# A matmul with a decayed running sum: w in four parts, the last group's upper half chunk by chunk, and output halves that rotate

## The chip, the core and the metric

The kernel runs on one core of one Trainium2 chip. The metric is the device time of an execution in microseconds (us); I quote medians of several executions. A profile is one execution, so its span can differ from the median by a us or two (932.1 against 934.55 for the kernel before). A ratio is the mean time of one kernel's runs over the mean time of the kernel before in the same rounds on the same chip, so it is not quite the ratio of the medians that I quote. Engines in the profile: PE is TensorE (matmul), PEld its weight loads, DVE VectorE, ACT ScalarE, POOL GpSimd, SP SyncE.

## The reference

```python
B, S, D = (16, 2048, 1024)
xw = x @ w
out[:, 0, :] = xw[:, 0, :]
for t in range(1, S):
    out[:, t, :] = decay[None, :] * out[:, t - 1, :] + xw[:, t, :]
```

## The kernel before: the parts that matter

The 16 x 2048 rows of x are cut into 64 chunks of 512 time steps, and chunks go in groups of two. A chunk is loaded by GpSimd's DMA queue, which casts to bf16 (the queue counts 68.18 MB for x and half of w, half of their 136.3 MB in f32), turned by a 32x32 transpose on VectorE ("turn", 2.3 us), and copied to matmul layout, mostly by ScalarE ("part"). TensorE then makes eight output tiles per group, n = 0 to 7, each from eight slots k of w. Behind each tile, ScalarE, GpSimd and VectorE do the recurrence (three tiles of four on every second time step, "paired", with a `scan` on half the steps), and VectorE transposes the result back into the output buffer `ot`, from which SyncE stores.

What the change touches is the start, the end and `ot`:

```python
groups = [[c, c + 1] for c in range(0, nch - 2, 2)] + [[nch - 2], [nch - 1]]

def ot_tile():
    return ring(sb, "ot", 2, [128, 2 * NJ, CQ])       # both halves of the columns
# ... cut ...
def lower(m):                                         # w's lower columns, f32, SyncE
    for q in range(NQ):
        pin(nc.sync.dma_start(out=stage[quad(q), m],
            in_=_ap(w, [[2 * D, P], [D, 2], [1, CH]], (q * CQ + m * 2 * P) * D)))
def upper(m):                                         # upper columns, cast to bf16, GpSimd
    for q in range(NQ):
        pin(nc.gpsimd.dma_start(out=stage2[quad(q), m], in_=...))
# ... cut ...
lower(0)
# decay: eight strided loads from ScalarE's queue
# x chunk 0 in two halves
for m in range(1, M):
    lower(m)
# x chunk 1 in two halves
for m in range(M):
    upper(m)
# ... cut ...
for m in range(M):
    at(m // 2, settle, m, 1, [nc.vector.tensor_copy] * 2)   # upper half into matmul layout
# ... cut ...
loads.extend((c, q) for c in (2, 3, 4) for q in range(NQ))  # later chunks, between GpSimd's adds
```

Of the kernel before, what the change touches and what calls it, by code (L numbers as in the profile page):

```python
# [25 lines left out]
def kernel(  # L26
# [25 lines left out]

    nc = tc.nc
# [4 lines left out]
    NQ = 4  # L58
# [26 lines left out]
    groups = [[c, c + 1] for c in range(0, nch - 2, 2)] + [[nch - 2], [nch - 1]]  # L85
    for g in groups:
        assert chunks[g[0]][0] == chunks[g[-1]][0]
# [6 lines left out]
    def ot_tile():  # L94
        return ring(sb, "ot", 2, [128, 2 * NJ, CQ])
# [29 lines left out]
    def matmul(ps, n, k, xt, t0=0, t1=TL):  # L125
        pin(nc.tensor.matmul(  # L126
            out=ps[:, t0:t1],
            lhsT=wsb[:, k, n].rearrange("p q i -> p (q i)"),
            rhs=xt[:, k // 2, k % 2, t0:t1],
            start=(k == 0),  # L130
            stop=(k == K - 1),
        ))
# [3 lines left out]
    class Tile:  # L136
# [3 lines left out]
        def __init__(self, gi, n, ps, ot):  # L140
            g = groups[gi]
# [3 lines left out]
            self.final = gi + 1 == len(groups)  # L145
            if len(g) == 2:
                self.paired = n % 4 != 3
            else:
                self.paired = n % 2 == 0 and not (self.final and n == K - 2)
# [65 lines left out]
        def back(self):  # L215
            T, n = self.T, self.n
            pin(nc.vector.transpose(  # L217
                out=self.ot[:, :, n * P:(n + 1) * P],
                in_=self.so[:, 2:T + 2].rearrange("p (i t) -> p i t", t=P)))
            if n == 3:  # L220
                self.store(0, 4)
            elif n == 5 and self.final:
                self.store(4, 6)
            elif n == 7:
                self.store(6 if self.final else 4, 8)

        def store(self, n0, n1):
            for q in (0, 2, 1, 3):
                pin(nc.sync.dma_start(
                    out=_ap(out, [[D, P], [P * D, self.T // P], [1, (n1 - n0) * P]],  # L230
                            (self.b * S + self.t0) * D
                            + n0 // R * CH + q * CR + n0 % R * P),
                    in_=self.ot[quad(q), :, n0 * P:n1 * P]))


    room = ot_tile().rearrange("p j c -> p (j c)")
    stage = room[:, 0:K * CH].rearrange("p (m e d) -> p m e d", m=M, e=2)
    stage2 = room[:, K * CH:K * CH * 3 // 2].bitcast(BF16).rearrange(
        "p (m e d) -> p m e d", m=M, e=2)

    def lower(m):
        for q in range(NQ):
            pin(nc.sync.dma_start(
                out=stage[quad(q), m],
                in_=_ap(w, [[2 * D, P], [D, 2], [1, CH]], (q * CQ + m * 2 * P) * D)))

    def upper(m):
        for q in range(NQ):
            pin(nc.gpsimd.dma_start(  # L249
                out=stage2[quad(q), m],  # L250
                in_=_ap(w, [[2 * D, P], [D, 2], [1, CH]], (q * CQ + m * 2 * P) * D + CH)))

    def settle(m, h, copies):
        for e, copy in enumerate(copies):
            src = (stage, stage2)[h][:, m, e]
            pin(copy(out=wcols[:, 2 * m + e, h],  # L256
                     in_=src.rearrange("p (q r i) -> p q r i", q=NQ, r=R)))

    def cast(m):
        settle(m, 0, (nc.vector.tensor_copy, nc.scalar.copy))  # L260

    idle = const.tile([128, TL], BF16, name="idle")
    spare = ring(psp, "spare", 1, [128, TL])
    pin(nc.vector.memset(idle, 0.0))  # L264
    for _ in range(40):
        pin(nc.tensor.matmul(out=spare, lhsT=idle[:, 0:128], rhs=idle, start=True, stop=True))  # L266
    H = NJ // 2
    halves = ((0, H), (H, NJ))
    lower(0)
    with nc.allow_non_contiguous_dma(reason="a vector of 1024"):  # L270
        for q in range(NQ):
            for h in range(2):
                pin(nc.scalar.dma_start(
                    out=dec[quad(q), h * R:(h + 1) * R],
                    in_=_ap(decay, [[1, P], [P, R]], h * CH + q * CR)))
# [3 lines left out]
    pin(nc.gpsimd.memset(stage[:, 1:M, 0, 0:1], 0.0))  # L279
    for m in range(1, M):  # L280
        lower(m)
# [3 lines left out]
    for m in range(M):  # L285
        upper(m)
# [6 lines left out]
    for m, (j0, j1) in enumerate(halves):  # L293
        enter(0, j0, j1)
        cast(m)
    for m in range(2, M):
        cast(m)
    pin(nc.vector.tensor_tensor(out=dec2[:, 0:K], in0=dec, in1=dec, op=ALU.mult))
    for j0, j1 in halves:
        enter(1, j0, j1)  # L300

# [12 lines left out]
    for m in range(M):  # L314
        at(m // 2, settle, m, 1, [nc.vector.tensor_copy] * 2)
    steps = {2: (3, 3, 4), 3: (4, 5, 6), 4: (7, 8, 10), nch - 1: (-11, -10, -8)}
    for gi, g in enumerate(groups):
        for l, c in enumerate(g):
            if c > 1:
                ahead = (-7, -6, -4) if l or len(g) == 1 else (-11, -10, -8)  # L320
                ahead = [gi * K + s for s in ahead]
                when = steps.get(c, ahead)
                if c == nch - 1:
                    when = [gi * K + s for s in when]
# [25 lines left out]
    loads.extend((c, q) for c in (2, 3, 4) for q in range(NQ))  # L350
    for gi, g in enumerate(groups):
        T = TL * len(g)
        if len(g) == 2:
            ot = ot_tile()
        else:
            if g[0] == nch - 2:
                both = ot_tile()
            ot = both[:, g[0] % 2 * NJ:(g[0] % 2 + 1) * NJ]
        heads = []
        if gi == 0:  # L360
            heads = [ring(psp, "ps", 3, [128, T]) for _ in range(3)]
            firsts = [ps[:, 0:TL] for ps in heads] + [spare]
            for k in range(K):
                for n in range(R):
                    matmul(firsts[n], n, k, xt_of[0])
            for j0, j1 in halves:
                for n in range(2):
                    for k in range(K):
                        matmul(heads[n][:, TL:T], n, k, xt_of[1], j0 * P, j1 * P)
        for n in range(K):  # L370
            if gi == 0 and n < R:
                if n < 3:
                    ps, second = heads[n], heads[n][:, TL:T]
                else:
                    second = ring(psp, "ps", 3, [128, TL])
                    ps = (spare, second)
                if n >= 2:
                    for k in range(K):
                        matmul(second, n, k, xt_of[1])
            else:  # L380
                if len(g) == 2 or n % 4 < 3:
                    ps = ring(psp, "ps", 3, [128, T])
                else:
                    ps = ring(psp, "spare", 1, [128, TL])
                for k in range(K):
                    for l, c in enumerate(g):
                        matmul(ps[:, l * TL:(l + 1) * TL], n, k, xt_of[c])
            behind(Tile(gi, n, ps, ot))
            for f in agenda.pop(gi * K + n, []):
                f()  # L390
            for _ in range(2 if len(loads) > NQ else 1):
                if loads:
                    load(*loads.pop(0))
# [31 lines left out]
```

## Time and profile before

| | before |
|---|---|
| median of four executions | 934.55 us (932.65 to 934.96) |
| span of the profiled one | 932.1 us |
| first useful matmul | 14.74 us |
| last matmul ends | 920.5 us |
| from there to the end of the span | 11.6 us |
| GpSimd's queue carries | x and half of w: 68.18 MB |
| SyncE's queue carries | half of w and all stores: 136.33 MB |

TensorE works without a gap from about 168 us to 920 us. The time is therefore decided before 168 us and after 920 us.

### The profile page before, as it was taken

The numbers are of one execution on the slowest core, as the hardware profiler recorded it, in microseconds if no ns is written. First come the engines' busy times: TensorE is split into PE (matmuls) and PEld (weight loads), VectorE is DVE, ScalarE is ACT, GpSimd is POOL, SyncE is SP. The second block draws the span as 40 slices with busy tenths as digits, with TensorE's granted clock in tenths as the row PEclk, the third lists the DMA queues.
The fourth block names the chain that finished last, engine by engine and source line by source line (L and its number), as shares of the span: only waits on it lengthen the run. The fifth ranks groups of instructions, "written<-read, shape, count | busy, mean of one in ns | idle before, by whom it ended". The sixth has DMA issues, their size and how long they took to land. (4 is left out here: it accounts for less than half of the span.)

```text
span 932.1 us, 11965 instructions
## 1 busy us (share of the span) xinstructions
PE 902.6 (97%) x4152; PEld 407.6 (44%) x4152; DVE 829.5 (89%) x613; ACT 685.9 (74%) x945; POOL 668.2 (72%) x767
## 2 busy tenths in 40 slices
PE   7879999999999999999999999999999999999995
PEld 2424444444444444444444444444444444444442
DVE  2869997999999999999999999999999999998997
ACT  2368877777877877877877777787787787787662
POOL 5867877777677777767777777777877777775542
PEclk9989999999999999999999999999999999999998
DMA  9899999999999999999999999999999999999678
GB/s 187 109 185 200 215 220 235 244 248 248 248 246 253 234 225 228 232 223 235 227 223 233 227 224 233 232 222 231 229 229 229 229 234 222 229 231 192 156 170 192
DMA packets 407548, 205.27 MB, mean 220 GB/s; under 512 B 14272, under 2 KB 406464, under 8 KB 407488
## 3 DMA queue, kind: packets, MB, share of 16 engines
q1 hardware_dynamic: 269760, 136.33, 59.9%
q0 software_dynamic: 136576, 68.18, 55.1%
q8 instruction: 32, 0.52, 0.2%
q10 hardware_dynamic: 1152, 0.00, 0.1%
q14 instruction: 28, 0.23, 0.1%
HBM read 138.42 MB, written 134.22 MB: 292 GB/s over the span
## 5 line engine op out<-in xcount | busy, mean ns | idle before, releaser
L126 PE MATMUL ps<-xt,wsb 128*128 128x512 bf16 x4072 | 883.8, 380 | 16.7 <-DVE wsb L256 5.2
L126 PEld LDWEIGHTS <-wsb 128*128 128x128 bf16 x4112 | 403.1, 98 | 504.7 <-issue 19.9
L176 POOL TENSOR_TENSOR xs<-h,xs 128x512 f32<-128x512 f32 (+1 forms) x193 | 246.8, 1279 | 194.2 <-ACT h L160 89.5
L217 DVE STREAM_TRANSPOSE ot<-so 128x1024 f32<-128x1024 f32 (+1 forms) x264 | 302.8, 1184 | 10.1 <-DMA out_dram<-ot 7.5
L170 ACT COPY xs<-ps 128x1024 f32<-128x1024 f32 (+1 forms) x193 | 192.2, 996 | 153.6 <-PE ps L126 150.9
L210 POOL TENSOR_TENSOR so<-h,xs 128x512 f32<-128x512 f32 (+1 forms) x193 | 245.6, 1273 | 47.4 <-ACT h L160 24.0
L123 ACT COPY xt<-xw 128x2048 bf16<-128x2048 bf16 (+1 forms) x128 | 240.0, 1876 | 18.2 <-DVE xw L115 18.2
L160 ACT ACTIVATE h<-so,dec 128x512 f32<-128x512 f32 (+1 forms) x193 | 147.6, 765 | 51.5 <-DVE so L182 47.7
L105 POOL DMA_DIRECT2D xb<-in_x_dram x264 | 174.6, 662 | 4.8 <-DMA xb<-in_x_dram 2.4
L115 DVE STREAM_TRANSPOSE xw<-xb 128x2048 f32<-128x2048 f32 (+1 forms) x66 | 146.7, 2222 | 14.3 <-DMA xb<-in_x_dram 14.2
L182 DVE TENSOR_TENSOR_SCAN so<-dec,xs 128x512 f32<-128x512 f32 x96 | 117.2, 1221 | 33.5 <-POOL xs L176 30.3
L182 DVE TENSOR_TENSOR_SCAN so<-dec,keep,xs 128x512 f32<-128x512 f32 (+1 forms) x97 | 120.1, 1238 | 29.9 <-POOL xs L176 29.8
L160 ACT ACTIVATE h<-ps,dec 128x512 f32<-128x512 f32 (+1 forms) x193 | 132.3, 686 | 0.0
L196 DVE TENSOR_TENSOR_SCAN so<-dec,keep,ps 128x1024 f32<-128x1024 f32 (+1 forms) x35 | 75.8, 2169 | 0.0
L196 DVE TENSOR_TENSOR_SCAN so<-dec,ps 128x1024 f32<-128x1024 f32 x31 | 70.1, 2261 | 0.0
L213 ACT COPY keep<-so 128x1 f32<-128x1 f32 x136 | 25.4, 187 | 0.2 <-DVE so L196 0.2
L175 ACT COPY so<-keep 128x1 f32<-128x1 f32 x97 | 18.5, 191 | 0.0
L249 POOL DMA_DIRECT2D ot<-in_w_dram x16 | 9.2, 579 | 6.9 <-DMA xb<-in_x_dram 6.7
L266 PE MATMUL spare<-idle 128*128 128x512 bf16 x40 | 11.5, 461 | 1.2 <-DVE idle L264 1.2
L173 POOL MEMSET so<- 128x1 f32 x96 | 11.3, 118 | 0.0
L126 PE MATMUL spare<-xt,wsb 128*128 128x512 bf16 x40 | 10.6, 379 | 0.0
L256 DVE CAST wsb<-ot 128x512 bf16<-128x512 f32 x4 | 1.7, 427 | 7.9 <-DMA ot<-in_w_dram 7.9
(15 smaller groups left out, 25.9 us busy)
## 6 DMA issues: line engine op xcount, KB each, us to landing
out_dram<-ot SPq DMA_DIRECT2D x248, 512.0 KB, 10.1
xb<-in_x_dram POOLq DMA_DIRECT2D x248, 256.0 KB, 7.6
out_dram<-ot SPq DMA_DIRECT2D x12, 256.0 KB, 4.2
ot<-in_w_dram SPq DMA_DIRECT2D x16, 128.0 KB, 6.5
xb<-in_x_dram POOLq DMA_DIRECT2D x16, 128.0 KB, 7.7
ot<-in_w_dram POOLq DMA_DIRECT2D x16, 64.0 KB, 3.0
out_dram<-ot SPq DMA_DIRECT2D x8, 128.0 KB, 2.7
dec<-in_decay_dram ACTq DMA_DIRECT2D x8, 0.5 KB, 4.7
```

Source lines behind the costliest of these rows:

```text
L105: pin(nc.gpsimd.dma_start(out=xb_of[c][quad(q), j0:j1], in_=_ap(x, [[D, P], [P * D, j1 - j0], [1, CQ]], (b * S + t0 + j0 * P) * D + q * CQ)))
L115: pin(nc.vector.transpose(out=dst.rearrange("p (m j i) -> p j m i", m=M, i=P)[:, j0:j1], in_=src.rearrange("p (j m c) -> p j m c", m=M, c=P)))
L123: pin(copy(out=xt_of[c][:, m0:m1, :, j0 * P:j1 * P], in_=src))
L126: pin(nc.tensor.matmul(out=ps[:, t0:t1], lhsT=wsb[:, k, n].rearrange("p q i -> p (q i)"), rhs=xt[:, k // 2, k % 2, t0:t1], start=(k == 0), ...
L160: pin(nc.scalar.activation(out=h, in_=src, func=mybir.ActivationFunctionType.Copy, scale=dec[:, self.n:self.n + 1]))
L170: pin(nc.scalar.copy(out=self.xs, in_=self.ps))
L176: pin(nc.gpsimd.tensor_tensor(out=self.xs[:, 1:T:2], in0=g, in1=self.xs[:, 1:T:2], op=ALU.add))
L182: pin(nc.vector.tensor_tensor_scan(out=so[:, 3:T + 2:2], data0=dec2[:, n:n + 1].to_broadcast([128, T // 2]), data1=self.xs[:, 1:T:2], init ...
L196: pin(nc.vector.tensor_tensor_scan(out=so[:, t:t + size], data0=dec[:, n:n + 1].to_broadcast([128, size]), data1=ps, initial=before, op0=A ...
L210: pin(nc.gpsimd.tensor_tensor(out=so[:, 2:T + 2:2], in0=h, in1=self.xs[:, 0:T:2], op=ALU.add))
L213: pin(nc.scalar.copy(out=self.keep, in_=so[:, T + 1:T + 2]))
L217: pin(nc.vector.transpose(out=self.ot[:, :, n * P:(n + 1) * P], in_=self.so[:, 2:T + 2].rearrange("p (i t) -> p i t", t=P)))
```

## The change

The intent: the first matmuls need only half of w's slots and half a chunk of x; w comes as (lower, even slots) by SyncE, then (lower, odd), (upper, even) and (upper, odd) by GpSimd in between the chunks of x, each part in four large loads. Decay comes contiguous, after w's first part. The third chunk of x is loaded before GpSimd's first add. Each half of the output columns has its own buffer. The last group is a pair for its lower columns and single chunks for its upper ones. A GpSimd memset that kept SyncE's later pieces of w behind the first loads of x (it ran at 6.01 us) goes. The diff, cut to its core:

```diff
-    groups = [[c, c + 1] for c in range(0, nch - 2, 2)] + [[nch - 2], [nch - 1]]
+    groups = [[c, c + 1] for c in range(0, nch, 2)]
-    def ot_tile():
-        return ring(sb, "ot", 2, [128, 2 * NJ, CQ])
+    def ot_tile(nj):
+        return ring(sb, "ot", 4, [128, nj, CR])
...
+    def load_w(queue, h, e):
+        for q in range(NQ):
+            pin(queue.dma_start(
+                out=stage[h, e][quad(q)].rearrange("p (m d) -> p m d", m=M),
+                in_=_ap(w, [[2 * D, P], [2 * P * D, M], [1, CH]],
+                        (q * CQ + e) * D + h * CH)))
...
-    for _ in range(40):
+    for _ in range(34):
...
-    lower(0)
-    (eight strided loads of decay by ScalarE)
+    load_w(nc.sync, 0, 0)
+    (four contiguous loads of decay by SyncE, into rows)
     (x chunk 0, two halves)
-    pin(nc.gpsimd.memset(stage[:, 1:M, 0, 0:1], 0.0))
-    for m in range(1, M):
-        lower(m)
+    load_w(nc.gpsimd, 0, 1)
     (x chunk 1, two halves)
-    for m in range(M):
-        upper(m)
+    load_w(nc.gpsimd, 1, 0)
+    load_w(nc.gpsimd, 1, 1)
+    for q in range(NQ):
+        load(2, q)
...
-        at(m // 2, settle, m, 1, [nc.vector.tensor_copy] * 2)
+        at(0, settle, 1, 1, m, nc.vector.tensor_copy)
-    steps = {2: (3, 3, 4), 3: (4, 5, 6), 4: (7, 8, 10), nch - 1: (-11, -10, -8)}
+    steps = {2: (3, 3, 4), 3: (4, 5, 5), 4: (7, 8, 10)}
...
-    loads.extend((c, q) for c in (2, 3, 4) for q in range(NQ))
+    loads.extend((c, q) for c in (3, 4) for q in range(NQ))
+    slots = [(g, n) for g in groups[:-1] for n in range(K)]
+    slots += [(groups[-1], n) for n in range(R)]
+    slots += [([c], n) for c in groups[-1] for n in range(R, K)]
...
+            for j0, j1 in halves:
+                for k in range(0, K, 2):
+                    for i in range(R):
+                        matmul(firsts[i], i, k, xt_of[0], j0 * P, j1 * P)
+            for k in range(1, K, 2):
+                for i in range(R):
+                    matmul(firsts[i], i, k, xt_of[0])
```

More of the change, by code (lines that the diff above doesn't have):

```diff
@@ L84 @@
     nch = len(chunks)
-    groups = [[c, c + 1] for c in range(0, nch - 2, 2)] + [[nch - 2], [nch - 1]]
+    groups = [[c, c + 1] for c in range(0, nch, 2)]
     for g in groups:
-        assert chunks[g[0]][0] == chunks[g[-1]][0]
+        assert chunks[g[0]][0] == chunks[g[1]][0]
     dec = const.tile([128, K], FP32, name="dec")
@@ L123, in part, with matmul @@
         pin(copy(out=xt_of[c][:, m0:m1, :, j0 * P:j1 * P], in_=src))
-    def matmul(ps, n, k, xt, t0=0, t1=TL):
+    def matmul(ps, n, k, xt, t0=0, t1=TL, start=0):
         pin(nc.tensor.matmul(
@@ L129, in matmul @@
             rhs=xt[:, k // 2, k % 2, t0:t1],
-            start=(k == 0),
+            start=(k == 0 and t0 == start),
             stop=(k == K - 1),
@@ L136, with __init__ @@
     class Tile:
-        def __init__(self, gi, n, ps, ot):
-            g = groups[gi]
+        def __init__(self, g, n, ps, ot):
             self.b, self.t0 = chunks[g[0]]
@@ L144, in __init__ @@
             self.n, self.ps, self.ot = n, ps, ot
-            self.final = gi + 1 == len(groups)
+            self.final = g == [nch - 1]
             if len(g) == 2:
-                self.paired = n % 4 != 3
+                self.paired = n % R != R - 1
             else:
@@ L217, in back @@
             pin(nc.vector.transpose(
-                out=self.ot[:, :, n * P:(n + 1) * P],
+                out=self.ot[:, :, n % R * P:(n % R + 1) * P],
                 in_=self.so[:, 2:T + 2].rearrange("p (i t) -> p i t", t=P)))
-            if n == 3:
-                self.store(0, 4)
-            elif n == 5 and self.final:
-                self.store(4, 6)
-            elif n == 7:
-                self.store(6 if self.final else 4, 8)
+            if self.final:
+                if n % 2:
+                    self.store(n - 1, n + 1)
+            elif n % R == R - 1:
+                self.store(n + 1 - R, n + 1)
@@ L227, in store @@
         def store(self, n0, n1):
+            c0 = n0 % R * P
+            size = (n1 - n0) * P
             for q in (0, 2, 1, 3):
                 pin(nc.sync.dma_start(
-                    out=_ap(out, [[D, P], [P * D, self.T // P], [1, (n1 - n0) * P]],
-                            (self.b * S + self.t0) * D
-                            + n0 // R * CH + q * CR + n0 % R * P),
-                    in_=self.ot[quad(q), :, n0 * P:n1 * P]))
-    room = ot_tile().rearrange("p j c -> p (j c)")
-    stage = room[:, 0:K * CH].rearrange("p (m e d) -> p m e d", m=M, e=2)
@@ L238 @@
-    stage2 = room[:, K * CH:K * CH * 3 // 2].bitcast(BF16).rearrange(
-        "p (m e d) -> p m e d", m=M, e=2)
-    def lower(m):
-        for q in range(NQ):
-            pin(nc.sync.dma_start(
-                out=stage[quad(q), m],
-                in_=_ap(w, [[2 * D, P], [D, 2], [1, CH]], (q * CQ + m * 2 * P) * D)))
-    def upper(m):
-        for q in range(NQ):
-            pin(nc.gpsimd.dma_start(
-                out=stage2[quad(q), m],
-                in_=_ap(w, [[2 * D, P], [D, 2], [1, CH]], (q * CQ + m * 2 * P) * D + CH)))
@@ L253, in settle @@
-    def settle(m, h, copies):
-        for e, copy in enumerate(copies):
-            src = (stage, stage2)[h][:, m, e]
-            pin(copy(out=wcols[:, 2 * m + e, h],
-                     in_=src.rearrange("p (q r i) -> p q r i", q=NQ, r=R)))
-    def cast(m):
-        settle(m, 0, (nc.vector.tensor_copy, nc.scalar.copy))
+                    out=_ap(out, [[D, P], [P * D, self.T // P], [1, size]],
+                            (self.b * S + self.t0) * D + n0 // R * CH + q * CR + c0),
+                    in_=self.ot[quad(q), :, c0:c0 + size]))
@@ new lines @@
+    room = [ot_tile(2 * NJ).rearrange("p j c -> p (j c)") for _ in range(2)]
+    size = M * CH
+    stage = {(0, 0): room[0][:, 0:size],
+             (0, 1): room[0][:, size:size * 3 // 2].bitcast(BF16),
+             (1, 0): room[1][:, 0:size // 2].bitcast(BF16),
+             (1, 1): room[1][:, size // 2:size].bitcast(BF16)}
+    def load_w(queue, h, e):
+        for q in range(NQ):
+            pin(queue.dma_start(
+                out=stage[h, e][quad(q)].rearrange("p (m d) -> p m d", m=M),
+                in_=_ap(w, [[2 * D, P], [2 * P * D, M], [1, CH]],
+                        (q * CQ + e) * D + h * CH)))
@@ L262, with settle @@
+    def settle(h, e, m, copy):
+        src = stage[h, e][:, m * CH:(m + 1) * CH]
+        pin(copy(out=wcols[:, 2 * m + e, h],
+                 in_=src.rearrange("p (q r i) -> p q r i", q=NQ, r=R)))
     idle = const.tile([128, TL], BF16, name="idle")
     spare = ring(psp, "spare", 1, [128, TL])
+    rows = const.tile([128, 2, P], FP32, name="rows")
     pin(nc.vector.memset(idle, 0.0))
-    for _ in range(40):
+    pin(nc.vector.memset(rows, 0.0))
+    for _ in range(34):
         pin(nc.tensor.matmul(out=spare, lhsT=idle[:, 0:128], rhs=idle, start=True, stop=True))
@@ L268 @@
     halves = ((0, H), (H, NJ))
-    lower(0)
-    with nc.allow_non_contiguous_dma(reason="a vector of 1024"):
-        for q in range(NQ):
-            for h in range(2):
-                pin(nc.scalar.dma_start(
-                    out=dec[quad(q), h * R:(h + 1) * R],
-                    in_=_ap(decay, [[1, P], [P, R]], h * CH + q * CR)))
+    load_w(nc.sync, 0, 0)
+    for q in range(NQ):
+        pin(nc.sync.dma_start(
+            out=rows[q * P:q * P + R],
+            in_=_ap(decay, [[P, R], [CH, 2], [1, P]], q * CR)))
     for j0, j1 in halves:
@@ L291, in enter @@
         part(c, nc.scalar.copy, 2, M, j0, j1)
-    for m, (j0, j1) in enumerate(halves):
-        enter(0, j0, j1)
-        cast(m)
-    for m in range(2, M):
-        cast(m)
+    for e in range(2):
+        for m in range(M):
+            settle(0, e, m, nc.vector.tensor_copy if m < M // 2 else nc.scalar.copy)
+        if e == 0:
+            for j0, j1 in halves:
+                enter(0, j0, j1)
+    cols = const.tile([128, 2, P], FP32, name="cols")
+    pin(nc.vector.transpose(out=cols, in_=rows))
+    pin(nc.vector.tensor_copy(
+        out=dec.rearrange("p (h r) -> p h r", h=2), in_=cols[:, :, 0:R]))
     pin(nc.vector.tensor_tensor(out=dec2[:, 0:K], in0=dec, in1=dec, op=ALU.mult))
@@ L300 @@
         enter(1, j0, j1)
+    for m in range(M):
+        settle(1, 0, m, nc.vector.tensor_copy)
     agenda = {}
@@ L319 @@
             if c > 1:
-                ahead = (-7, -6, -4) if l or len(g) == 1 else (-11, -10, -8)
-                ahead = [gi * K + s for s in ahead]
-                when = steps.get(c, ahead)
-                if c == nch - 1:
-                    when = [gi * K + s for s in when]
+                ahead = (-7, -6, -4) if l else (-11, -10, -8)
+                when = steps.get(c, [gi * K + s for s in ahead])
                 at(when[0], turn_and_load, c)
@@ L348, in behind @@
                 tl.back()
-    loads.extend((c, q) for c in (2, 3, 4) for q in range(NQ))
-    for gi, g in enumerate(groups):
-        T = TL * len(g)
-        if len(g) == 2:
-            ot = ot_tile()
-        else:
-            if g[0] == nch - 2:
-                both = ot_tile()
-            ot = both[:, g[0] % 2 * NJ:(g[0] % 2 + 1) * NJ]
-        heads = []
-        if gi == 0:
+    loads.extend((c, q) for c in (3, 4) for q in range(NQ))
+    slots = [(g, n) for g in groups[:-1] for n in range(K)]
@@ L361 @@
+    slots += [(groups[-1], n) for n in range(R)]
+    slots += [([c], n) for c in groups[-1] for n in range(R, K)]
+    for step, (g, n) in enumerate(slots):
+        T = TL * len(g)
+        if n % R == 0:
+            ot = ot_tile(NJ * len(g))
+        if step == 0:
             heads = [ring(psp, "ps", 3, [128, T]) for _ in range(3)]
             firsts = [ps[:, 0:TL] for ps in heads] + [spare]
-            for k in range(K):
-                for n in range(R):
-                    matmul(firsts[n], n, k, xt_of[0])
@@ L366 @@
-            for j0, j1 in halves:
-                for n in range(2):
-                    for k in range(K):
-                        matmul(heads[n][:, TL:T], n, k, xt_of[1], j0 * P, j1 * P)
-        for n in range(K):
-            if gi == 0 and n < R:
-                if n < 3:
-                    ps, second = heads[n], heads[n][:, TL:T]
-                else:
-                    second = ring(psp, "ps", 3, [128, TL])
-                    ps = (spare, second)
-                if n >= 2:
-                    for k in range(K):
-                        matmul(second, n, k, xt_of[1])
-            else:
-                if len(g) == 2 or n % 4 < 3:
-                    ps = ring(psp, "ps", 3, [128, T])
-                else:
-                    ps = ring(psp, "spare", 1, [128, TL])
-                for k in range(K):
-                    for l, c in enumerate(g):
-                        matmul(ps[:, l * TL:(l + 1) * TL], n, k, xt_of[c])
-            behind(Tile(gi, n, ps, ot))
-            for f in agenda.pop(gi * K + n, []):
-                f()
-            for _ in range(2 if len(loads) > NQ else 1):
-                if loads:
-                    load(*loads.pop(0))
+            for j0, j1 in halves:
+                for k in range(0, K, 2):
+                    for i in range(R):
+                        matmul(firsts[i], i, k, xt_of[0], j0 * P, j1 * P)
@@ new lines @@
+            for k in range(1, K, 2):
+                for i in range(R):
+                    matmul(firsts[i], i, k, xt_of[0])
+            for j0, j1 in halves:
+                for i in range(2):
+                    for k in range(K):
+                        matmul(heads[i][:, TL:T], i, k, xt_of[1], j0 * P, j1 * P, j0 * P)
+        if step < R:
+            if n < 3:
+                ps, second = heads[n], heads[n][:, TL:T]
+            else:
+                second = ring(psp, "ps", 3, [128, TL])
+                ps = (spare, second)
+            if n >= 2:
+                for k in range(K):
+                    matmul(second, n, k, xt_of[1])
+        else:
+            if len(g) == 2 or n % R < 3:
+                ps = ring(psp, "ps", 3, [128, T])
+            else:
+                ps = ring(psp, "spare", 1, [128, TL])
+            for k in range(K):
+                for l, c in enumerate(g):
+                    matmul(ps[:, l * TL:(l + 1) * TL], n, k, xt_of[c])
@@ L394 @@
+        behind(Tile(g, n, ps, ot))
+        for f in agenda.pop(step, []):
+            f()
+        for _ in range(2 if len(loads) > NQ else 1):
+            if loads:
+                load(*loads.pop(0))
     behind(None)
```

## The prediction

The sum came to 2.65 + 4.4 = 7 us, and 934.4 - 7 = 927.4. "Cold matmuls": those with weight loads some 0.43 us apart; the trace has 23 of them (0.38 to 0.43), between 38 and 65 us, where the text says some 28, so 5 us rather than 6.

> **What bounds the kernel now.** I read the page first, then the TensorE timeline, then the timeline of all engines over the first 75 us, last the chain that ended last. The page:
>
> ```profile
> PE 902.6 (97%) x4152; PEld 407.6 (44%) x4152; DVE 829.5 (89%) x613; ACT 685.9 (74%) x945; POOL 668.2 (72%) x767
> ...
> L126 PE MATMUL ps<-xt,wsb 128*128 128x512 bf16 x4072 | 883.8, 380 | 16.7 <-DVE wsb L256 5.2
> ```
>
> TensorE is busy 97% of the 932.1 us span. The work is 64 chunks x 8 outputs x 8 slots = 4096 matmuls of 512 columns. Their pace comes from two ScalarE copies that wait for TensorE four output tiles (64 matmuls) apart, at 868.81 and 882.57 us: 13.76 / 64 = 0.215 us. So 4096 of them need 881 us, and only the other 51 us are to be had. The TensorE timeline says where those are (start, length, then in brackets the idle time before and who ended it):
>
> ```profile
> 1.20 11.54 PE L266 MATMUL spare<-idle 128*128 128x512 bf16 x40 [1.20 <-DVE idle L264]
> 14.74 0.81 PE L126 MATMUL ps<-xt,wsb 128*128 128x512 bf16 x3 [2.00 <-DVE xt L123]
> ...
> 36.34 1.04 PE L126 MATMUL ps<-xt,wsb 128*128 128x512 bf16 x4 [1.99 <-DVE wsb L256]
> 37.82 5.56 PE L126 MATMUL ps<-xt,wsb 128*128 128x512 bf16 x18 [0.45 <-DVE wsb L256]
> 43.69 3.61 PE L126 MATMUL ps<-xt,wsb 128*128 128x512 bf16 x16 [0.31 <-DVE so L196]
> 50.45 5.51 PE L126 MATMUL ps<-xt,wsb 128*128 128x512 bf16 x17 [3.15 <-ACT h L160]
> 56.90 1.89 PE L126 MATMUL ps<-xt,wsb 128*128 128x512 bf16 x8 [0.93 <-ACT xt L123]
> ```
>
> ```profile
> 60.92 20.65 PE L126 MATMUL ps<-xt,wsb 128*128 128x512 bf16 x87 [2.14 <-ACT xt L123]
> 83.29 83.04 PE L126 MATMUL ps<-xt,wsb 128*128 128x512 bf16 x384 [1.72 <-DVE so L196]
> 167.53 62.75 PE L126 MATMUL ps<-xt,wsb 128*128 128x512 bf16 x290 [1.20 <-DVE so L196]
> ```
>
> The first useful matmul starts at 14.74. Gaps up to 61 us sum to about 12 (those shown are 9; 1.09, 1.65 and a rest before 25 us are waits for casts of w), then 1.7 and 1.2, then none. After gaps the weight loads stand 0.43 us apart instead of 0.215 for some 28 matmuls, 28 x 0.21 = 6 us more. At the other end TensorE stops at 920.5, and the tail is 11.6 us. Sum: 14.7 + 881 + 12 + 6 + 2.9 + 11.6 = 928, 4 short of 932, so the terms are good to a few us. The cause of the early gaps:
>
> ```profile
> 12.07 0.62 ACT L256 CAST wsb<-ot 128x512 bf16<-128x512 f32 x1 [0.56 <-DMA ot<-in_w_dram]
> 12.71 1.25 DVE L115 STREAM_TRANSPOSE xw<-xb 128x1024 f32<-128x1024 f32 x1 [0.21 <-DMA xb<-in_x_dram]
> ...
> 32.17 5.59 DVE L256 COPY wsb<-ot 128x512 bf16<-128x512 bf16 x4
> ...
> 47.00 1.90 ACT L123 COPY xt<-xw 128x2048 bf16<-128x2048 bf16 x1 [4.98 <-DVE xw L115]
> ...
> 68.70 2.31 DVE L115 STREAM_TRANSPOSE xw<-xb 128x2048 f32<-128x2048 f32 x1 [4.42 <-DMA xb<-in_x_dram]
> ```
>
> The first part of w lands at 12.07, the second half of x's first chunk at 12.71. Four copies of w's upper half keep VectorE from 32.2 to 37.8; everything behind them is late, so ScalarE waits 5 us for a transpose and TensorE then 3 us for ScalarE. At 68.7 VectorE has waited for the fifth chunk of x. The chain ends thus:
>
> ```profile
> 923.91 1.16 DVE so L196
> 925.08 0.60 DVE ot L217
> 925.68 0.59 DVEq L420
> ```
>
> [...] casts of w's four pieces of 0.5 MB wait until 12.07, 15.41, 18.93 and 22.48, 3.5 us each, 150 GB/s, while the second chunk's 1 MB (as bf16) lands between 12.7 and 22.9, about 100 GB/s. Counted from the packet records, SyncE's queue moved about 90 KB and GpSimd's 35 KB per half us from 11 to 16 us, and GpSimd's alone 95 KB. Between 3 and 10 us SyncE's got far less: only two pieces were issued by 3.8 us, as SyncE waited for the decay loads (1.9 us in its waits).
> [...] the eight bf16 copies of w last 274, 286 and 3840 ns (least, median, most), and the longest lies from 32.44 to 36.28 under GpSimd adds and DMA issues.
> [...]
>
> **The change, part by part.**
> (1) SyncE's first loads become four of 256 KB (even slots, lower columns, 1 MB), with nothing to wait for; decay comes after, contiguous, and is transposed on chip. At the rates above w's part has 128 KB by 3 us and the other 0.9 MB at 180 KB per us by 8, landed about 8.8. Meanwhile x gets 70 KB per us, 350 of its first half's 512 KB; the rest at 190 KB per us ends at 9, and lands 1.3 us later, as now, at 10.3. VectorE: two casts of 0.43 in that wait, turn 1.25, copy 0.69: first matmul at 12.25, against 14.74: 2.5 us won. The 34 warm-up matmuls (14 at 0.43, 20 at 0.21) end at 11.4, just before.
> (2) Everything behind it comes through GpSimd's queue, 0.5 MB per 2.75 us, each part landing 1.2 us after its data: x second half 13.0; odd slots of w 15.7; second chunk 18.5 and 21.2; upper even 24.0, upper odd 26.7; third chunk 32.3. Today upper w takes until about 31, in 16 issues of 0.53 us that hold that queue to 64 KB per issue; now 8 issues of 128 KB.
> TensorE then: half-chunk matmuls 12.25 to 14.0, gap 1.0, to 16.7; odd slots to 20.2; gap 0.25, to 22.2; gap 0.95, to 24.9; outputs 2 and 3 to 28.3. That is about 3.5 us before today's 31.8. Matmul columns are unchanged.
> (3) Output 4 needs the upper copies. If they pass, they end about 28.9, 8.8 us before today's 37.8, and output 4 hardly waits. Behind them, by today's durations: scan 1.2, ScalarE 0.8, copy and decay of the next tile 1.7: output 5 at 32.7, output 6 at 38.4 after VectorE's two scans, output 7 at 45.5 (today 50.45), because ScalarE still waits for the third chunk's turn, which VectorE reaches only at 39.6. The next group begins about 52.1 (today 56.9), its two copies back to back, so the 2.1 us gap at 60.92 goes.
> (4) The fifth chunk's load is issued one chunk earlier, so VectorE does not idle 4.4 us at 68.7. VectorE ends the scan of output 7 about 60.5 (today 63.15), 2.65 won, and then turns that chunk without a wait: 2.65 + 4.4 = 7 us won. VectorE is 89% busy and holds the PSUM buffers, so it fixes what remains: 7 us, not TensorE's 8 at the start of group two.
> (5) Output halves rotate through four tiles of the same total size. Waits of VectorE for stores are 7.5 us in two places, and cost TensorE 1.2. I put 0.
> (6) The last group: lower half as a pair, upper half by chunk. The last four tiles (two paired, two not), the two narrow stores and the order behind TensorE's end stay the same, and TensorE has no gap near the end. I put 0.
> Sum: 7 us of 934.4 makes 927.4.
>
> **The rivals.** A: [...] In the new order the last upper copies become ready at 26.7, just as GpSimd starts its first add (h ready at 25.75, after the third chunk's issues)[...]. Then output 4 stops for 2 us and all behind is 2.7 later: gain 4, time 930. For it: the 3840 ns copy; against: four copies ran undisturbed under DMA issues at 26.7. B: the first load starves under x as it does today (SyncE's third piece waited 3.5 us): first matmul at 14 to 15, casts late, gain 3 to 5, time 930. C: the early waits nearly all vanish [...]: a 881 us pace with 12 us start, 11.6 tail and 8 of stalls gives a span of 913 to 917, time 915 to 919; against it, the third chunk's turn sits behind seven VectorE instructions. D: the tail shortens or lengthens: less backlog of stores could give 1 us.
>
> **Range and chances.** A and B pull towards 930, C towards 918; centre 927, range 919 to 933. A gain of over 2% needs 18.7 us, nearly all the 20 us of early gaps and cold matmuls: 4%. Over 2% slower needs a new standing wait where VectorE or stores fall behind: 1%. Within 2%: 95%.
>
> **What would show it.** First useful matmul at about 12.2 (step 1); upper w's last copy near 28.9 and no copy of several us (step 3, rival A); output 7 near 45.5; no wait for x near 68 (step 4); after 100 us the same pace of 0.215; TensorE's end to the end of the span 11.6 (step 6). I am wrong if the pace of the middle changes, or if TensorE waits for stores.

## The result, and the profile after

The changed kernel takes 928.15 us (928.14 to 928.26, four runs) against 934.55; ratio 0.9936, 95% interval 0.9919 to 0.9953. It is a clear gain of 6 us (4.4 to 7.6 by the interval, at 934). A second set of six runs gave 928.20. The kernel before is the less steady one: its executions lie between 932.25 and 938.53, those of the changed kernel between 928.09 and 928.66.

The profiled span went from 932.1 to 926.5, 5.6 us less, and that is a sum of two terms of opposite sign:

| | before | after | difference |
|---|---|---|---|
| first useful matmul | 14.74 | 12.81 | -1.9 |
| last matmul ends | 920.5 | 912.5 | -8.0 |
| last matmul to end of span | 11.6 | 14.0 | +2.4 |
| span | 932.1 | 926.5 | -5.6 |

The start first. This is the timeline of all engines of the changed kernel, as in the prediction:

```profile
8.83 0.77 DVE L253 CAST wsb<-ot 128x512 bf16<-128x512 f32 x2 [7.61 <-DMA ot<-in_w_dram]
...
10.79 1.25 DVE L116 STREAM_TRANSPOSE xw<-xb 128x1024 f32<-128x1024 f32 x1 [1.19 <-DMA xb<-in_x_dram]
...
26.88 3.69 DVE L253 COPY wsb<-ot 128x512 bf16<-128x512 bf16 x4 [1.52 <-DMA ot<-in_w_dram]
...
62.04 2.27 DVE L116 STREAM_TRANSPOSE xw<-xb 128x2048 f32<-128x2048 f32 x1
```

w's first part is there at 8.83, before the first half of x; the last part at 26.88, where the kernel before had its last copies from 32 to 38. The fifth chunk is turned at 62.04 with no bracket behind the row: its data were there before VectorE was free. The kernel before waited 4.42 us for it until 68.70. TensorE's timeline of the changed kernel after the first 30 us:

```profile
34.13 3.61 PE L127 MATMUL ps<-xt,wsb 128*128 128x512 bf16 x16 [1.75 <-ACT h L160]
40.25 1.12 PE L127 MATMUL ps<-xt,wsb 128*128 128x512 bf16 x4 [2.51 <-DVE so L196]
41.60 3.95 PE L127 MATMUL ps<-xt,wsb 128*128 128x512 bf16 x11 [0.22 <-issue]
47.01 3.83 PE L127 MATMUL ps<-xt,wsb 128*128 128x512 bf16 x17 [1.46 <-ACT h L160]
52.93 6.92 PE L127 MATMUL ps<-xt,wsb 128*128 128x512 bf16 x30 [2.08 <-ACT xt L124]
```

```profile
61.03 13.97 PE L127 MATMUL ps<-xt,wsb 128*128 128x512 bf16 x63 [1.19 <-DVE so L196]
76.61 827.23 PE L127 MATMUL ps<-xt,wsb 128*128 128x512 bf16 x3755 [1.60 <-DVE so L196]
```

Read these against the rows of the kernel before: the waits for copies of w at 36 and 38 us are gone, output 7 starts at 47.01 (before 50.45), the next group at 52.93 (before 56.90). The second wait for a copy, 2.14 us at 60.92, is gone; a wait of 1.19 us for VectorE stands at 61.03. The last early gap ends at 76.61 (before 83.29). The 1.2 us gap at 167.5 has no counterpart. (Records of some matmuls are missing from a trace, 4080 beside 4162 weight loads on the changed kernel's page, so a short stretch can look idle; where a neighbouring engine's rows do not agree, I don't count it.)

A rival for the gain is the clock: the granted clock was 0.64, 0.64 and 0.65 from 38 to 42, 50 to 54 and 62 to 66 us in the kernel before, and in the changed kernel only 0.88 and 0.69 from 38 to 46. A second profile of the changed kernel (the run "once more" below) had a granted clock of 1.00 all the way from 34 to 78 us. Its tiles start at the same times to 0.01 us, and TensorE ends at 912.5 in both. Its row for output 7:

```profile
47.02 3.83 PE L127 MATMUL ps<-xt,wsb 128*128 128x512 bf16 x17 [3.15 <-ACT h L160]
```

So the slower matmuls of the first profile (weight loads 0.43 us apart from 41.2 to 44.2 us, 0.22 before and after) only shortened the wait behind them, from 3.15 to 1.46 us: this stretch at half pace costs nothing. The gap ahead of it was of the same length in both profiles (2.51 and 2.52 us, at 40.3), so its length did not decide the clock. The three stretches of the kernel before have no such check.

The end. The chain that ended last, changed kernel:

```profile
916.26 1.16 DVE so L196
917.42 0.60 DVE ot L217
918.02 0.59 DVEq L419
```

VectorE's last transpose ends at 918.6, about as long after the last matmul as before (6.1 us against 5.8). But then it is 7.9 us to the end of the span, where it was 5.8. Only stores are left there. The table of stretches shows them; columns are the stretch, its length, the five engines' busy time (with counts), the granted TensorE clock, the DMA engines' busy share, and GB/s. Kernel before, where TensorE ends at 920.5:

```profile
916.00:920.00 4.00, 4.00 (x20) 1.84 (x19) 3.70 (x6) 1.45 (x4) 1.47 (x2) 1.00 0.60 151
920.00:924.00 4.00, 0.52 (x3) 0.02 (x1) 4.00 (x6) 0.52 (x1) 0.73 (x1) 1.00 0.80 184
924.00:928.00 4.00, 0.00 (x0) 0.00 (x0) 2.27 (x3) 0.00 (x0) 0.00 (x0) 0.62 0.96 210
928.00:932.00 4.00, 0.00 (x0) 0.00 (x0) 0.00 (x0) 0.00 (x0) 0.00 (x0) 0.50 0.61 130
```

The changed kernel, where it ends at 912.5:

```profile
904.00:908.00 4.00, 4.00 (x21) 1.75 (x19) 3.70 (x5) 1.64 (x6) 1.13 (x2) 1.00 0.42 81
908.00:912.00 4.00, 4.00 (x20) 1.84 (x19) 3.70 (x6) 1.63 (x6) 1.82 (x3) 1.00 0.94 201
912.00:916.00 4.00, 0.47 (x3) 0.00 (x0) 4.00 (x6) 0.52 (x1) 0.73 (x1) 0.86 0.99 253
916.00:920.00 4.00, 0.00 (x0) 0.00 (x0) 2.61 (x4) 0.00 (x0) 0.00 (x0) 0.50 0.98 258
920.00:924.00 4.00, 0.00 (x0) 0.00 (x0) 0.00 (x0) 0.00 (x0) 0.00 (x0) 0.50 0.99 204
924.00:928.00 4.00, 0.00 (x0) 0.00 (x0) 0.00 (x0) 0.00 (x0) 0.00 (x0) 0.50 0.26 54
```

Before, the DMA engines had a 0.60 share just ahead of TensorE's end: the stores had run dry and were waiting for new tiles. After, they ran dry earlier (a share of 0.42 from 904 to 908 us) and are full from 908 us almost to the end (0.94 to 0.99 up to 924). GB/s times length, from TensorE's end on: before 3.5 x 184 + 4 x 210 + 4 x 130 = 2.0 MB, after 3.5 x 253 + 4 x 258 + 4 x 204 + 4 x 54 = 2.95 MB. Nearly 1 MB more was still to be stored.

### The profile page after: what moved, and what is told of

It is laid out like the page before. It is cut to its first block, busy times and chain, and to the rows that moved or that the text cites. A ratio compares the mean times of both kernels' runs of the same rounds, so it can differ in the third digit from the quotient of the medians.

```text
span 926.5 us, 11865 instructions
## 1 busy us (share of the span) xinstructions
PE 893.3 (96%) x4080; PEld 408.1 (44%) x4162; DVE 827.9 (89%) x608; ACT 686.2 (74%) x937; POOL 666.6 (72%) x760
## 3 DMA queue, kind: packets, MB, share of 16 engines
q0 software_dynamic: 137024, 68.70, 55.4%
## 5 line engine op out<-in xcount | busy, mean ns | idle before, releaser
L127 PE MATMUL ps<-xt,wsb 128*128 128x512 bf16 (+1 forms) x4018 | 879.1, 378 | 18.0 <-DVE so L196 5.3
L176 POOL TENSOR_TENSOR xs<-h,xs 128x512 f32<-128x512 f32 x192 | 247.4, 1288 | 206.0 <-ACT h L160 95.4
L170 ACT COPY xs<-ps 128x1024 f32<-128x1024 f32 x192 | 193.0, 1005 | 163.7 <-PE ps L127 155.5
L210 POOL TENSOR_TENSOR so<-h,xs 128x512 f32<-128x512 f32 x192 | 246.5, 1284 | 34.8 <-ACT h L160 22.4
L160 ACT ACTIVATE h<-so,dec 128x512 f32<-128x512 f32 x192 | 147.8, 770 | 39.3 <-DVE so L182 35.7
L160 ACT ACTIVATE h<-ps,dec 128x512 f32<-128x512 f32 x192 | 132.5, 690 | 0.0
L262 PE MATMUL spare<-idle 128*128 128x512 bf16 x34 | 10.3, 479 | 1.2 <-DVE idle L259 1.2
L246 POOL DMA_DIRECT2D ot<-in_w_dram x12 | 6.7, 560 | 4.2 <-DMA xb<-in_x_dram 2.7
L253 DVE COPY wsb<-ot 128x512 bf16<-128x512 bf16 x10 | 5.4, 595 | 2.8 <-DMA ot<-in_w_dram 2.8
## 6 DMA issues: line engine op xcount, KB each, us to landing
out_dram<-ot SPq DMA_DIRECT2D x252, 512.0 KB, 10.3
```

The lines of the kernel that those rows point to most:

```text
L127: pin(nc.tensor.matmul(out=ps[:, t0:t1], lhsT=wsb[:, k, n].rearrange("p q i -> p (q i)"), rhs=xt[:, k // 2, k % 2, t0:t1], start=(k == 0 a ...
L160: pin(nc.scalar.activation(out=h, in_=src, func=mybir.ActivationFunctionType.Copy, scale=dec[:, self.n:self.n + 1]))
L170: pin(nc.scalar.copy(out=self.xs, in_=self.ps))
L176: pin(nc.gpsimd.tensor_tensor(out=self.xs[:, 1:T:2], in0=g, in1=self.xs[:, 1:T:2], op=ALU.add))
L210: pin(nc.gpsimd.tensor_tensor(out=so[:, 2:T + 2:2], in0=h, in1=self.xs[:, 0:T:2], op=ALU.add))
```

## The experiments

Twelve kernels ran, each with five rounds beside the kernel before (six executions of each, four of the two that say so). The three calls of four fell on three chips, so kernels of one call compare best; the changed kernel's own median was 928.15 on the first occasion and 928.20 in the first call here, and it did not run in the two others. I name an effect by the difference of medians to 928.2 and give the ratio to the kernel before beside it. Across calls that difference can be off by some tenths of a us: the kernel before had medians of 933.73, 934.11 and 934.28 in the three. The theory after the first reading of the traces: (a) the start won 8 us through earlier copies of w and an earlier fifth chunk, less one long copy of w on VectorE (2.47 us); (b) the new order of the last group piles up stores and gives 2.4 us back. The main rivals: the tail is a matter of the engines' chain, or of any earlier end; and the start's gain comes from the first matmul's earlier begin.

**The changed kernel once more.**

> The changed kernel itself, as the yardstick of this call. 928 us, TensorE ends at 912.5 and the span ends 14.0 us later. A second run that disagrees by over 1.5 us would mean that the parts below cannot be told apart.

928.20 us (928.09 to 928.66), ratio 0.9931. It repeats within 0.05 us.

**The old end on the changed kernel.**

```diff
-    groups = [[c, c + 1] for c in range(0, nch, 2)]
+    groups = [[c, c + 1] for c in range(0, nch - 2, 2)] + [[nch - 2], [nch - 1]]
-            if self.final:
+            if self.final and n >= R:
-                ahead = (-7, -6, -4) if l else (-11, -10, -8)
+                ahead = (-7, -6, -4) if l or c == nch - 2 else (-11, -10, -8)
-    slots = [(g, n) for g in groups[:-1] for n in range(K)]
-    slots += [(groups[-1], n) for n in range(R)]
-    slots += [([c], n) for c in groups[-1] for n in range(R, K)]
+    slots = [(g, n) for g in groups for n in range(K)]
```

> The changed kernel with the last two chunks as before, each whole and on its own. Theory stores: the pair's lower half puts 2 MB of stores at once 13.8 us before TensorE's end, so that 4 MB instead of 3 MB are left for the last 14 us; undone, the tail goes from 14.0 back to 11.6 us with TensorE ending at 912.5 as in the changed kernel: 925.7, 0.9974 of it. Rival: the longer tail is the chain of the last tiles on VectorE and GpSimd, or the earlier end of TensorE itself; then it stays near 14 and the time at 928.

926.15 us (925.76 to 926.64), ratio 0.9909: 2.05 us faster than the changed kernel of the same call. TensorE ends at 912.24, the span at 924.1: a tail of 11.9 us. Its stretches:

```profile
908.00:912.00 4.00, 4.00 (x20) 1.74 (x18) 3.70 (x7) 1.46 (x4) 1.47 (x2) 1.00 0.54 134
912.00:916.00 4.00, 0.24 (x2) 0.00 (x0) 4.00 (x6) 0.52 (x1) 0.73 (x1) 0.98 0.89 209
916.00:920.00 4.00, 0.00 (x0) 0.00 (x0) 1.97 (x3) 0.00 (x0) 0.00 (x0) 0.50 0.89 197
920.00:924.00 4.00, 0.00 (x0) 0.00 (x0) 0.00 (x0) 0.00 (x0) 0.00 (x0) 0.50 0.55 120
```

The 0.54 share before the end is back, and the tail with it, although TensorE ends as early as in the changed kernel. The rival of the early end falls.

**The new end on the kernel before.** The same edit, the other way round, with the kernel before's buffers (the pair's lower tiles and the single chunks' upper tiles share its output buffer).

> The kernel before with the new order of the last group alone. Theory stores: TensorE ends where it did (920.5) and the tail goes from 11.6 to 14.0 us, so 2.1 to 2.4 us slower than the kernel before, 1.0024 of it. Rival: the longer tail needs the new start, and the time is within 0.5 of the kernel before.

937.10 us (935.74 to 939.18), ratio 1.0032, interval 1.0015 to 1.0048: 3 us slower. TensorE ends at 920.3, where it did, and the span at 934.3: a tail of 14.0 us. Two of its stretches, around TensorE's end and the last:

```profile
916.00:920.00 4.00, 4.00 (x20) 1.76 (x18) 3.70 (x6) 1.64 (x6) 1.66 (x3) 1.00 0.94 203
932.00:936.00 4.00, 0.00 (x0) 0.00 (x0) 0.00 (x0) 0.00 (x0) 0.00 (x0) 0.50 0.25 53
```

So the new end costs 2 to 3 us in either kernel, in both by the tail. Why, by counting stores in the code: the pair's lower half is 2 MB that can only be stored when its fourth tile is done, and eight single tiles of 1.72 us, 13.8 us in all, follow it on TensorE; then come 1 MB and twice 0.5 MB, 4 MB from there on. In the old order 1 MB of that had been stored a chunk's half earlier, and 3 MB are left.

**Two of the last four copies of w on ScalarE.**

```diff
-        at(0, settle, 1, 1, m, nc.vector.tensor_copy)
+        at(0, settle, 1, 1, m, nc.vector.tensor_copy if m < 2 else nc.scalar.copy)
```

> The changed kernel with two of the last four copies of w (upper half, odd slots) on ScalarE instead of VectorE. [...] the third copy lay 2.47 us under two GpSimd adds and held the first scan from 28.0 to 30.5; without it the scan starts at 28.0, output 5 at 32.4 instead of 34.1, and TensorE ends 1.5 to 2 us earlier: about 926.3. Rival absorbed: the later waits (output 7 on ScalarE's copies, the PSUM buffers that VectorE holds) take it all back, and the time stays within 0.5 of 928.

927.09 us (926.80 to 927.70), ratio 0.9920: 1.1 us faster, less than the 1.5 to 2 expected. VectorE's timeline of this kernel:

```profile
27.59 0.70 DVE L253 COPY wsb<-ot 128x512 bf16<-128x512 bf16 x2 [2.46 <-DMA ot<-in_w_dram]
28.22 1.21 DVE L182 TENSOR_TENSOR_SCAN so<-dec,xs 128x512 f32<-128x512 f32 x1
31.62 1.23 DVE L182 TENSOR_TENSOR_SCAN so<-dec,xs 128x512 f32<-128x512 f32 x1 [2.18 <-POOL xs L176]
```

The text says two adds; the changed kernel's trace has two DMA issues and one add of GpSimd over the long copy. The first scan starts at 28.22 instead of 30.49: the long copy did hold VectorE, for 2.3 us. That GpSimd's work made it long is read from the overlap (its 27.89 to 30.36 lie over GpSimd's 27.56 to 30.20), and not tested by itself. The second scan gains nothing at first, since ScalarE's two copies delay the tile that it waits for, and the rest of the gain goes through. Part of the miss is of another kind: in this execution w's last part landed 0.7 us later (27.59 against 26.88).

**The old output buffer on the changed kernel.**

```diff
-        return ring(sb, "ot", 4, [128, nj, CR])
+        return ring(sb, "ot", 2, [128, nj, CQ])
-                out=self.ot[:, :, n % R * P:(n % R + 1) * P],
+                out=self.ot[:, :, n * P:(n + 1) * P],
```

> The changed kernel with the output buffer as before: two tiles of both halves instead of four of one half. The first transpose into a tile then waits for all eight stores of the group before last, not for four. Theory rotation matters a little: VectorE waits for stores again in one to three places, several us each, and TensorE loses about 1.2 us there (as at 167.5 in the kernel before): 929 to 930. Rival: stores are early enough everywhere, 0 within 0.3.

928.30 us (928.02 to 928.97), ratio 0.9933: nothing, as the rival said. The program does show the difference that the rotation makes: the first transpose into a buffer waits for four stores instead of all eight. But here it cost VectorE one wait of 1.57 us at 124.8, and TensorE no gap. The kernel before had a wait of 5.94 us for stores at 162.94, followed by TensorE's 1.2 us gap at 167.5; this kernel, with the same buffer, has neither. The kernel before with the new end (above) has the old buffer and the old start. It waits for stores there too, 4.29 us at 162.28, and has no gap behind it. So the wait went with the start, not with the buffer; which part of the start removed it stays open, and the gap is no fixed cost of the old kernel.

**The third chunk's load back between the adds.**

```diff
-    for q in range(NQ):
-        load(2, q)
-    loads.extend((c, q) for c in (3, 4) for q in range(NQ))
+    loads.extend((c, q) for c in (2, 3, 4) for q in range(NQ))
```

> The changed kernel with the third chunk's load not ahead of GpSimd's first add but between its adds as before, so that every later chunk is issued one chunk later. Step 4 of the prediction: the fifth chunk's last quarter is then issued about 53 us and lands about 65 beside the stores, VectorE waits 3 us or so for it, and as VectorE sets the pace there, TensorE ends about 3 us later: 930.5 to 931.5. Rival: VectorE has room to catch up, at most 0.5 us.

931.43 us (931.22 to 932.91), ratio 0.9973: 3.2 us slower by the medians. VectorE's timeline has the wait, and TensorE's what became of it:

```profile
65.61 2.31 DVE L116 STREAM_TRANSPOSE xw<-xb 128x2048 f32<-128x2048 f32 x1 [3.08 <-DMA xb<-in_x_dram]
```

```profile
71.41 837.07 PE L127 MATMUL ps<-xt,wsb 128*128 128x512 bf16 x3864 [2.90 <-ACT h L160]
```

This is the largest single part of the gain that an experiment took back: one chunk's load is issued earlier on GpSimd, because it no longer queues between that engine's adds.

**w's upper half in 16 loads of 64 KB.**

```diff
+        step = M if h == 0 else M // 2
+        for m in range(0, M, step):
             (four loads, each of step slots from m on)
```

> The changed kernel with w's upper half in 16 loads of 64 KB, as before, instead of 8 of 128 KB. Step 2 of the prediction: issues of 0.53 to 0.6 us then hold the queue to half its rate, the upper half lands 2.5 to 3 us later (about 29.5), output 4 waits for it and all behind is 2 to 3 us later: 930 to 931. Rival: the issue rate isn't what limits, or the time is absorbed by the wait of output 5 on ScalarE (1.75 us) and later ones: under 1 us.

929.69 us (929.42 to 930.00), ratio 0.9952: 1.5 us slower, half of what was expected. w's last part landed at 29.57 (2.7 us later, as expected), and its copies took 2.25 us there. But the first scan, at 31.74, is only 1.25 us later than in the changed kernel, where the copies had come earlier and taken longer (3.69 us). The longer copies hid half of the earlier landing.

**The first matmuls on whole chunks.**

```diff
-            for j0, j1 in halves:
-                for k in range(0, K, 2):
-                    for i in range(R):
-                        matmul(firsts[i], i, k, xt_of[0], j0 * P, j1 * P)
+            for k in range(0, K, 2):
+                for i in range(R):
+                    matmul(firsts[i], i, k, xt_of[0])
```

> The changed kernel with the even slots' first matmuls on whole chunks instead of halves, so that the first useful matmul waits for the second half of x: at 15.5 us instead of 12.8. Theory: the 2.7 us at the start are nearly worthless, because the first half of the second chunk, and its second half at 23.6 us, set TensorE's next start anyway: within 0.7 us of the changed kernel, 928.2 to 928.9. Rival, as step 1 of the prediction counted it: up to 2.5 us, 930.5.

928.69 us (927.86 to 929.89), ratio 0.9941: 0.5 us slower by the medians and 0.9 by the ratios (0.0010 of 934 us), neither clear of the noise, though the first useful matmul came at 15.43 instead of 12.81. An earlier first matmul is nearly worthless here, since TensorE only waits the more behind it: the changed kernel waits 0.82, 0.81 and 1.75 us for VectorE and ScalarE up to 34.13, this one has no gap from 15.43 to 38.04, and the next start is at 40.06 against 40.25.

**Decay as before.** Eight strided loads by ScalarE, at once, in place of four by SyncE after w's first part.

> The changed kernel with decay loaded as before: eight strided loads from ScalarE's queue, which share completion semaphores with SyncE's loads of w, so that three of w's four pieces wait for a decay load. Theory: w's first part lands 2 to 4 us later than 8.8 us, the first useful matmul comes 2 us later, but as with whole chunks most of that is taken up by the wait for the second chunk: 0.3 to 1.2 us slower, 928.5 to 929.4. Rival A: decay's wait is what made the kernel before slow to start: 3 us or more. Rival B: none, w lands when it did.

930.06 us (929.36 to 931.28), ratio 0.9954: 1.9 us slower, between the theory's 1.2 and rival A's 3. The expected step was far off, the time less so: w's first part landed at 14.19 instead of 8.83, 5.4 us later and not 2 to 4, and the first matmul came at 16.93. SyncE's waits and VectorE's timeline:

```profile
SPq L246 <- DMA dec<-in_decay_dram: 3.4, 2, 3.0
```

```profile
14.19 0.76 DVE L253 CAST wsb<-ot 128x512 bf16<-128x512 f32 x2 [13.04 <-DMA ot<-in_w_dram]
```

In the trace, loads of SyncE and of ScalarE raise the same semaphores at their end, and w's second piece waited for a load of decay that had the semaphore before it (number 107: decay's first load raises it, and the second piece, issued at 4.17, waits for it). SyncE's waits for decay sum to 3.4 us, 3.0 the longest. The kernel before shows one such wait, 1.9 us: its fourth piece of w waits for number 112, which decay's third load raises (107, 110, 113, 115 and 116 are raised by both too). The other 2 us are in the packet records: between 4 and 7 us, SyncE's queue moved nothing, although its pieces were issued from 4.2 us on, and GpSimd's moved 110 to 155 KB per us. From 8 to 12 us SyncE's moved 140 to 210 KB per us. The piece that was issued at 4.17 into the other queue's running stream moved its first packet at 7.13, 3.0 us later; in the changed kernel the first piece took 1.0 us (0.75 to 1.76). The kernel before has the same: its third piece was issued at 3.79, and from 5 to 7 us SyncE's queue moved 4 KB and GpSimd's 287.

**Both gains together.** The old end and the two copies on ScalarE.

> The changed kernel with the last two chunks whole, as before, and two of the four last copies of w on ScalarE. If the two gains (2.05 and 1.1 us) lie at the two ends and don't touch, they add: 925.0. Rival: they overlap, 926.

924.84 us (924.72 to 924.99), ratio 0.9896 (four executions). They add, as far as two calls can be compared.

**ScalarE's copy of the third chunk behind output 4's copies.**

```diff
-    steps = {2: (3, 3, 4), 3: (4, 5, 5), 4: (7, 8, 10)}
+    steps = {2: (3, 4, 4), 3: (4, 5, 5), 4: (7, 8, 10)}
```

> The one before, and the first copy of the third chunk's turned x on ScalarE put behind the copies that free output 4's PSUM buffer. ScalarE otherwise sits 5 us in front of it, and output 7 waits 3.15 us for that buffer. Theory: output 7 starts 3 us earlier, but the next group waits for the third and fourth chunk's copies, so that 1 us or so stays: 924.0. Rival: no gain, the next group starts when it did.

924.07 us (923.95 to 924.48), ratio 0.9888, interval 0.9871 to 0.9906 (four executions). This is the best kernel: 10 us faster than the kernel before and 4 us faster than the changed one. The 3.15 us wait of output 7 is gone, the next group waits 1.50 us for ScalarE to free a PSUM buffer and 2.62 us for its copy, and 0.8 us of the gain stays.

**Two of the last four stores by ScalarE.**

```diff
+                queue = nc.scalar if self.final and n0 == K - 2 and q % 2 else nc.sync
-                pin(nc.sync.dma_start(
+                pin(queue.dma_start(
```

> The one before, with two of the last four stores issued by ScalarE, which is idle by then, instead of all by SyncE. SyncE issues the last ones 0.6 us apart behind one another; two fewer take about 1 us off the tail: 923.0. Rival: the stores themselves, not their issue, set the end: 924.0.

931.03 us (930.39 to 934.05), ratio 0.9970: 7 us slower than the kernel without the edit, a clear miss. SyncE's waits from 890 us on:

```profile
SPq L231 <- DMA out_dram<-ot: 12.5, 1, 12.5
```

Two of the semaphores that SyncE's stores raise too (numbers 111 and 113 in the trace) went to ScalarE's stores, which were issued after the last transpose, from 915.33 on, and took 2.4 us to land. A store of SyncE's that comes earlier in the program waits for number 111 until 917.79, 12.5 us in all, for a store that is issued later in time. From 908 to 916 us the DMA engines moved nothing. Whether two queues would help without that isn't settled by this run.

## Why the prediction was right

The median, 928.15, is 1.2 us from the predicted 927, well inside 919 to 933. By its own steps:

1. **First part of w.** Predicted landed at 8.8 and x's half at 10.3, first matmul 12.25. Measured 8.83, 10.79 and 12.81. The landing of w held to 0.03 us, but partly by luck, since the rates behind it did not: by the packet records SyncE's queue had 294 KB by 3 us (predicted 128), then moved 149 to 174 KB per us up to 7 us (predicted 180), and x moved 45 KB per us from 4 to 7 us (predicted 70; 231 packets of 2 KB by SyncE's queue stand there beside 271 of 0.5 KB by GpSimd's), so x came half a us late. But the step's "2.5 us won" was not a gain of the whole: whole chunks give 2.6 us of it away and lose only 0.5. The prediction did not add it in, as its sum rests on VectorE. Rival B, a starved first load, did not come.
2. **The other parts.** Predicted upper even 24.0, upper odd 26.7; the copies that waited for them started at 24.14 and 26.88. Worth 1.5 us by the experiment with 16 loads.
3. **The copies pass.** They did not: rival A came true in part. The four copies took 3.69 us, where four undisturbed ones took 0.89 in the kernel before; one of them took 2.47 us (27.89 to 30.36), where GpSimd's timeline has two DMA issues (27.56 to 28.86) and an add (28.91 to 30.20); the first took 0.89 us, under an earlier add, and the four ended at 30.57, not 28.9 (the prediction does not say how its 26.7 becomes 28.9). Output 4 did not stop, as the rival had it: TensorE has no gap from 23.57 to 32.38. Output 5 began at 34.13 instead of 32.7, output 7 at 47.01 instead of 45.5, the next group at 52.93 instead of 52.1. The rival's 2.7 us were too much, since the waits of outputs 5 to 7 take part of it.
4. **The fifth chunk.** Predicted a turn without a wait right after output 7's scan (60.5) and one transpose (1.2), so at about 61.7: measured 62.04, 6.7 us before the old 68.70, where 7 were predicted. With the load put back, 3.2 us are lost. The step and its size hold; the rest of the 6.7 us is VectorE's earlier start on this tile.
5. **Rotation: 0.** Measured 0.1.
6. **The last group: 0.** This is the step that failed: +2.4 us in the profile, and 2.05 us in the run with the old end. The prediction looked at the order of instructions behind TensorE's end, which is the same, and at TensorE's gaps, of which there are none; it did not count the bytes of stores that the new order leaves for the last 14 us: 4 MB instead of 3. Rival D had named stores, with the wrong sign and 1 us.

The sum: 7 us for the start were 8.0 at TensorE's end, of which 1.2 are the gap at 167.5 of this one execution, and the tail took 2.4 back. So 7 was predicted, and 6.4 by the medians or 5.6 by the two profiles came, from two errors of opposite sign. That the total is so near is in part luck: a right total is no proof of each term. Of the start, single undoing gives 3.2 (early load), 1.9 (decay), 1.5 (large loads), 0.5 (half chunks) and 0.1 (rotation), 7.2 in sum, if they add, which was not tested. By the differences of the ratios they are 3.9, 2.1, 2.0, 0.9 and 0.2, 9.1 in sum, each good to some 1.5 us. Not undone singly: the order of w itself (even slots first, the odd ones by GpSimd), the memset that held w back, and the 34 matmuls on `idle` instead of 40.

## What to carry to other kernels

Where an engine is busy for 96 to 97% of the span, as TensorE here, count the bytes and the waits at the two ends: here the order of the loads was worth up to 3.2 us, and 1 MB of stores more behind the last matmuls cost 2. A larger tile to store held 2 MB back at the end; what larger tiles cost in the middle of a kernel was not tested. And before spreading DMAs over two issuing engines, look at what their completion semaphores make them wait for: here up to 12.5 us.
